# Squares of the residual in tiles of their own, in the output projection of a hybrid decoder layer

## The chip, the cores and the metric

One core of a Trainium2 chip runs the whole layer as one program. The metric is the device time of that program in microseconds (us), the median of three runs. The engines named below are PE (matrix products), DVE and ACT (elementwise work), POOL (hardly used) and SP (it issues most of the loads). An engine works through its own queue in order; ACT's queue also carries the DMA issues that ACT makes.

## What is computed

The layer has 512 tokens of width 2048. What matters here is its middle:

```python
x = x + ycat.reshape(B, S, D_MIX) @ w_out[l]          # four branches, joined, one output projection
h = rmsnorm(x, norm_ffn_g[l])                          # needs the sum of squares of x over the 2048 features
x = x + (silu(h @ w_gate[l]) * (h @ w_up[l])) @ w_down[l]
```

## The kernel before

Everything is kept transposed: a tile is 128 features by 512 tokens, and x is 16 such tiles, `x2[0]` to `x2[15]`. Float32 products are done with three matmuls of rounded parts: a value is split into `hi` (ACT, a copy that rounds) and `lo` (DVE, the rest), for weights (`issue_split`, L122 on ACT and L123 on DVE) as for data (`split2`, L1057 on ACT and L1058 on DVE).

The program order is written out by hand, and each engine keeps it. The output projection comes in two parts. The first (L1022) adds three branches to x. The second is the loop over `g` from 0 to 7 that the diff touches. Each `g` takes one weight chunk of 128x4x256 and computes two blocks of x, `g` and `g + 8`, here called a pair, with 24 matmuls (L162 to L164), 12 for a block. Before its matmuls `next_chunk` splits the chunk of the pair after it, so the split of chunk g+1 stands at the head of pair g in the queues of ACT and DVE, behind everything of pair g-1. The three raw weight buffers and four split buffers are shared by turns.

When a block is done, `on_last` runs `make_x2` (L1047): DVE adds the product to x2 (L1048), ACT scales it by the norm's gain into `xg` (L1050), ACT's queue issues a DMA that stores x2 to DRAM (`xd`, L1051; it is read again near the end of the layer), and ACT squares x2 in place (L1053). Behind the second block of a pair come `split_a11` (half of xg, rounded on ACT and subtracted on DVE), `add_squares` (L1043, DVE: one add of the two oldest tiles of squares), and `first_sums(g - 1)` (L1071, L1072, L1078 on DVE, with a split of the result between them: L1057 on ACT, L1058 on DVE). At g = 6 the first gate weights are split as well (`w_split(0)`).

Then come the gate and up projections, in 11 groups of weights, each by a recursive scheme of seven products P1, P5, P6, P3, P7, P4, P2 with 48 matmuls each, in four steps of 12 (`strassen`, L1244 to L1246). At each step DVE and ACT form sums of raw weights (`w_sum`, L1135 to L1147) and split them (`w_split`), two to three steps ahead. Between half steps the generators in `side` advance by one: `late_sums` makes the other sums of xg (first group only), and `ffn_norm` adds up the remaining tiles of squares, one add for each half step, then sums them over the partitions with matmuls against a column of ones (`norm2.add`, L229, on PE) and takes the root (L234, L235). The norm's factor `norm2.r` is first read at the end of P4 (L1202). The tiles named here come from one pool of 79 buffers.

The products P1, P6, P7 and P4 accumulate in the same PSUM banks, and the partial results are taken out in between: by ACT (L1199) after P1, P5 and P6, by DVE after P3 (L1211) and P7 (L1213). The next product on these banks waits for that.

Of the kernel before, what the change touches and what calls it, by code (L numbers as in the profile page):

```python
# [10 lines left out]
AF = mybir.ActivationFunctionType  # L11
# [28 lines left out]
def hybrid_kernel(ctx, tc, xT, wi, wt, wo, wgu, wdn, vec, rows, sgw, w2a2, g2, pbias, cmask, oneh, addc, out):  # L40
    nc = tc.nc
    pe, dv, ac, gp = nc.tensor, nc.vector, nc.scalar, nc.gpsimd
# [11 lines left out]
    def t2(name, shape=(128, 512), dt=F32):  # L54
        return p2.tile(list(shape), dt, name=name, tag="s2")
# [94 lines left out]
    def gemm(nchunk, rhs, on_block):  # L150

        acc = [None, None]
        for c in range(nchunk):
            hi, lo = next_chunk()
            for b in range(2):
                if c == 0:
                    acc[b] = pm(f"acc{b}")
                for k in range(4):
                    xh, xl = rhs(c, k)
                    wh = hi[:, k, b * 128:(b + 1) * 128]  # L160
                    wl = lo[:, k, b * 128:(b + 1) * 128]
                    pe.matmul(acc[b], wh, xh, start=(c == 0 and k == 0), stop=False)  # L162
                    pe.matmul(acc[b], wh, xl, start=False, stop=False)  # L163
                    pe.matmul(acc[b], wl, xh, start=False, stop=(c == nchunk - 1 and k == 3))  # L164
                if c == nchunk - 1:
                    on_block(b, acc[b])
                yield
# [49 lines left out]
    def vcol(i):  # L217
        return vc[:, i:i + 1]
# [732 lines left out]
    def run(g, n=1):  # L951
        for _ in g:
            step_side(n)
# [57 lines left out]
    x2 = {}  # L1011
# [25 lines left out]
    sqs = []  # L1037
    cmb = {}

    def add_squares(sqs=sqs, cc=slice(0, S)):  # L1040
        if len(sqs) > 1:
            t = sqs.pop(0)
            dv.tensor_add(sqs[0][:, cc], t[:, cc], sqs[0][:, cc])  # L1043
# [3 lines left out]
    def make_x2(j, acc):  # L1047
        dv.tensor_add(x2[j], acc, x2[j])  # L1048
        xg[j] = t2("xg")
        ac.activation(xg[j], x2[j], AF.Copy, scale=vcol(V_NFG + j))  # L1050
        nc.scalar.dma_start(xd[j], x2[j])  # L1051
        sqs.append(x2.pop(j))
        ac.activation(sqs[-1], sqs[-1], AF.Square)  # L1053

    def split2(hi, src, lo):

        ac.activation(hi, src, AF.Copy)  # L1057
        dv.tensor_sub(lo, src, hi.bitcast(F32))  # L1058

    def split_a11(j):  # L1060
        a11 = t2("a11", dt=F32R)
        split2(a11[:, lo_t], xg[j][:, lo_t], a11[:, hi_t])
        cmb["P1", j] = a11[:, lo_t], a11[:, hi_t]
# [3 lines left out]
    def first_sums(j):  # L1067

        a, b = xg[j], xg[j + 8]
        s12 = s2[j] = t2("s12")  # L1070
        dv.tensor_add(s12[:, lo_t], a[:, hi_t], b[:, hi_t])  # L1071
        dv.tensor_sub(s12[:, hi_t], s12[:, lo_t], a[:, lo_t])  # L1072
        h12, l12 = t2("h12", dt=F32R), t2("l12", dt=F32R)
        split2(h12, s12, l12)
        cmb["P5", j] = h12[:, lo_t], l12[:, lo_t]
        cmb["P6", j] = h12[:, hi_t], l12[:, hi_t]

        dv.tensor_sub(s12[:, lo_t], b[:, lo_t], s12[:, hi_t])  # L1078
# [21 lines left out]
    def ffn_norm():  # L1100
        while len(sqs) > 1:
            add_squares()
            yield
        norm2.add(sqs.pop(0))
        norm2.root()
        yield
# [10 lines left out]
    def w_dma(limit):  # L1117
        while sw["dma"] < min(limit, len(steps)):
            gi, p, jj = steps[sw["dma"]]
            if p in FRESH:  # L1120
                if len(raw) + 2 > RAWS:
                    return
                kh, f = FRESH[p]
                for j in (2 * jj, 2 * jj + 1):
                    t = raw[kh, f, j] = t2("wq")
                    nc.sync.dma_start(t, wgu[gi, kh, f, j])
            sw["dma"] += 1
# [21 lines left out]
    def w_split(k):  # L1149
        gi, p, jj = steps[k]  # L1150
        hi = wp.tile([128, 2, 512], F32R, name="wh", tag="wraw", bufs=3)
        lo = wp.tile([128, 2, 512], F32R, name="wl", tag="wsp", bufs=4)
        if p in ("P5", "P6", "P4"):
            split2(hi, src.pop(k), lo)
        else:
            for u, j in enumerate((2 * jj, 2 * jj + 1)):
                q = {"P1": (0, 0), "P3": (1, 1), "P7": (1, 1), "P2": (1, 0)}[p] + (j,)
                split2(hi[:, u], raw.pop(q) if p in ("P7", "P2") else raw[q], lo[:, u])
        cut[k] = hi, lo
# [96 lines left out]
    for g in range(8):  # L1256
        def on_last(b, acc, g=g):
            make_x2(g + 8 * b, acc)
            if b:
                split_a11(g)  # L1260
                add_squares()
                if g:
                    first_sums(g - 1)
                if g == 4:
                    w_dma(4)
                if g == 6:
                    w_split(0)
                    sw["add"] = sw["split"] = 1
        run(gemm(1, lambda c, k: (yh[0, k], yl[0, k]), on_last))
    for f in range(4):  # L1270
        del yh[0, f], yl[0, f]
    side.append(late_sums())
    side.append(ffn_norm())


# [181 lines left out]
```

## Time and profile before

| | us |
|---|---|
| median of 3 runs (2360.51 to 2361.64) | 2361.01 |
| the profiled execution | 2362.09 |
| its span | 2360.3 |
| PE busy | 2280.0 (97%) |
| DVE busy | 1408.9 (60%) |
| ACT busy | 934.1 (40%) |

A stretch of the trace is given in us from the start of the span. The loop over g runs from about 873 to 970; group 0 of the gate and up projections follows it. The granted clock (PEclk) is a share of TensorE's full speed: 1.00 is 2.4 GHz, 0.50 is 1.2 GHz. Rows of waits name the engine that waited, its line, and the work that ended the wait.

### The profile page before, as it was taken

What the parts mean: (1) busy time and instruction counts of PE and PEld (TensorE: products, weight loads), DVE (VectorE), ACT (ScalarE), POOL (GpSimd) and SP (SyncE); (2) the same over time, 40 slices, a digit from 0 to 9 for tenths busy, and PEclk for the clock granted to TensorE, in tenths of its full rate; (3) what the DMA queues carried; (4) which work ended last, traced back from release to release, by engine and by line L of the source; (5) the groups of instructions that cost most, each with busy time, mean ns of one, the idle gap of its engine ahead of it and who ended that gap; (6) DMA issues with size and microseconds to landing.
All of it is one profiled execution on the core that took longest, in us unless ns stands there. A gap on an engine that the chain in (4) does not pass through costs nothing.

```text
span 2360.3 us, 29410 instructions
## 1 busy us (share of the span) xinstructions
PE 2280.0 (97%) x11404; PEld 1844.0 (78%) x11404; DVE 1408.9 (60%) x2250; ACT 934.1 (40%) x1465; POOL 2.3 (0%) x16
## 2 busy tenths in 40 slices
PE   8999999999999995699999999999999899999997
PEld 6788878877777774478888888888888788888887
DVE  6555456654444443688687868787878534434336
ACT  5522222243454433354544554455445422222223
POOL 0000000000000000000000000000000000000000
PEclk9999999999999997799999999999999999999999
DMA  5232323233233233234454545354534534434332
GB/s 186 86 91 74 100 75 92 60 99 90 63 100 114 89 104 117 93 124 157 134 165 132 159 134 170 125 161 134 165 129 166 195 99 134 128 96 133 116 116 90
DMA packets 144379, 283.00 MB, mean 120 GB/s; under 512 B 26544, under 2 KB 43440, under 8 KB 144240
## 3 DMA queue, kind: packets, MB, share of 16 engines
q1 hardware_dynamic: 124208, 255.12, 34.6%
q10 hardware_dynamic: 20032, 26.01, 3.3%
q8 instruction: 89, 1.46, 0.3%
q14 instruction: 50, 0.41, 0.1%
HBM read 260.33 MB, written 20.75 MB: 119 GB/s over the span
## 4 chain that ended last, share of the span: by engine, by line
PE 89%; DVE 5%; DMA 3%; ACT 2%; issue 1%; ACTq 0%; SPq 0%; DVEq 0%
PE acc L162 13%; PE acc L164 13%; PE acc L163 13%; PE prod L1244 11%; PE prod L1246 11%; PE prod L1245 11%; PE acc L180 3%; PE acc L182 2%; PE acc L181 2%; DMA xd<-x 2%; DVE wl L1058 1%; PE ph L1187 1%; PE po L898 1%; PE psc L833 1%; PE ppt L848 1%; PE acc L1361 1%
## 5 line engine op out<-in xcount | busy, mean ns | idle before, releaser
L123 DVE TENSOR_TENSOR wlo<-wraw,whi 128x1024 fp32r<-128x1024 f32 x207 | 253.2, 1224 | 300.4 <-ACT whi L122 300.2
L122 ACT ACTIVATE whi<-wraw 128x1024 fp32r<-128x1024 f32 x207 | 218.8, 1057 | 537.4 <-PE acc L163 431.7
L1058 DVE TENSOR_TENSOR wl<-wq,wh 128x512 fp32r<-128x512 f32 x352 | 227.3, 688 | 116.0 <-ACT wh L1057 114.8
L1245 PE MATMUL prod<-wl,h 128*128 128x512 f32 x704 | 274.7, 390 | 0.8 <-DVE wl L1058 0.8
L1244 PE MATMUL prod<-wh,h 128*128 128x512 f32 x704 | 274.7, 390 | 0.0
L1246 PE MATMUL prod<-wh,l 128*128 128x512 f32 x704 | 274.4, 390 | 0.0
L1057 ACT ACTIVATE wh<-wq 128x512 fp32r<-128x512 f32 x352 | 201.4, 623 | 165.0 <-PE prod L1246 108.4
L162 PE MATMUL acc<-hhi,whi 128*128 128x512 f32 x640 | 250.3, 391 | 2.4 <-ACT whi L122 2.4
L164 PE MATMUL acc<-hhi,wlo 128*128 128x512 f32 x640 | 250.1, 391 | 0.0
L163 PE MATMUL acc<-hlo,whi 128*128 128x512 f32 x640 | 250.0, 391 | 0.0
L162 PE MATMUL acc<-xhi,whi 128*128 128x512 f32 x512 | 209.5, 409 | 5.1 <-ACT whi L137 5.1
L164 PE MATMUL acc<-xhi,wlo 128*128 128x512 f32 x512 | 201.1, 393 | 1.0 <-DVE wlo L123 1.0
L163 PE MATMUL acc<-xlo,whi 128*128 128x512 f32 x512 | 201.0, 393 | 0.3 <-DVE xlo L253 0.3
L1057 ACT ACTIVATE wh<-T 128x1024 fp32r<-128x1024 f32 x132 | 139.9, 1060 | 149.5 <-PE prod L1246 140.6
L1058 DVE TENSOR_TENSOR wl<-T,wh 128x1024 fp32r<-128x1024 f32 x132 | 161.6, 1224 | 41.9 <-ACT wh L1057 41.9
L1245 PEld LDWEIGHTS prod<-wl,h 128*128 128x128 f32 x704 | 132.6, 188 | 28.9 <-DVE wl L1058 1.3
L1246 PEld LDWEIGHTS prod<-wh,l 128*128 128x128 f32 x704 | 132.6, 188 | 27.6
L1244 PEld LDWEIGHTS prod<-wh,h 128*128 128x128 f32 x704 | 132.6, 188 | 27.5
L1244 PE MATMUL prod<-wh,hb 128*128 128x512 f32 x352 | 139.8, 397 | 6.7 <-DVE c L1213 6.7
L162 PEld LDWEIGHTS acc<-hhi,whi 128*128 128x128 f32 x640 | 120.8, 189 | 28.0 <-ACT whi L122 2.8
L164 PEld LDWEIGHTS acc<-hhi,wlo 128*128 128x128 f32 x640 | 120.7, 189 | 25.8 <-DVE wlo L123 0.8
L163 PEld LDWEIGHTS acc<-hlo,whi 128*128 128x128 f32 x640 | 120.8, 189 | 25.1
(284 smaller groups left out, 3841.4 us busy)
## 6 DMA issues: line engine op xcount, KB each, us to landing
wq<-in_wgu_dram SPq DMA_DIRECT2D x440, 256.0 KB, 3.3
wraw<-in_wdn_dram SPq DMA_DIRECT2D x88, 512.0 KB, 3.5
wraw<-in_wi_dram SPq DMA_DIRECT2D x63, 512.0 KB, 3.6
wraw<-in_wt_dram SPq DMA_DIRECT2D x32, 512.0 KB, 3.6
wraw<-in_wo_dram SPq DMA_DIRECT2D x32, 512.0 KB, 3.5
hd<-hT ACTq DMA_DIRECT2D x44, 256.0 KB, 3.4
hraw<-hd SPq DMA_DIRECT2D x44, 256.0 KB, 4.8
xraw<-in_xT_dram SPq DMA_DIRECT2D x16, 256.0 KB, 5.5
```

Source lines behind the costliest of these rows:

```text
L122: ac.activation(hi, r, AF.Copy)
L123: dv.tensor_sub(lo, r, hi.bitcast(F32))
L162: pe.matmul(acc[b], wh, xh, start=(c == 0 and k == 0), stop=False)
L163: pe.matmul(acc[b], wh, xl, start=False, stop=False)
L164: pe.matmul(acc[b], wl, xh, start=False, stop=(c == nchunk - 1 and k == 3))
L180: pe.matmul(acc[i], th_, hi[:, k], start=(c == 0 and k == 0), stop=False)
L181: pe.matmul(acc[i], th_, lo[:, k], start=False, stop=False)
L1057: ac.activation(hi, src, AF.Copy)
L1058: dv.tensor_sub(lo, src, hi.bitcast(F32))
L1244: pe.matmul(acc[t], ah[:, tt], hi[:, u], start=first, stop=False, skip_group_check=more)
L1245: pe.matmul(acc[t], ah[:, tt], lo[:, u], start=False, stop=False, skip_group_check=more)
L1246: pe.matmul(acc[t], al[:, tt], hi[:, u], start=False, stop=(j == 7), skip_group_check=more)
```

## The change

Squaring leaves `make_x2` and becomes a function of its own that writes a new tile and lets go of x2. It is called for both blocks of a pair behind `split_a11` and `first_sums`; the add of squares comes last, and not at g = 0. In `ffn_norm` eight empty half steps stand between the last add and the matmuls of the column sums.

```diff
@@ make_x2
         ac.activation(xg[j], x2[j], AF.Copy, scale=vcol(V_NFG + j))
         nc.scalar.dma_start(xd[j], x2[j])
-        sqs.append(x2.pop(j))
-        ac.activation(sqs[-1], sqs[-1], AF.Square)
+
+    def square_x2(j):
+        sqs.append(t2("sq"))
+        ac.activation(sqs[-1], x2.pop(j), AF.Square)
@@ ffn_norm
         while len(sqs) > 1:
             add_squares()
             yield
+        for _ in range(8):
+            yield
         norm2.add(sqs.pop(0))
         norm2.root()
@@ on_last
             make_x2(g + 8 * b, acc)
             if b:
                 split_a11(g)
-                add_squares()
                 if g:
                     first_sums(g - 1)
+                square_x2(g)
+                square_x2(g + 8)
+                if g:
+                    add_squares()
                 if g == 4:
                     w_dma(4)
```

## Rows read from the trace of the kernel before

**Rows 1.** Windows: each engine's busy us (instructions), granted clock, DMA share, GB/s.

```profile
873.00:970.43 97.43, 60.03 (x193) 42.81 (x191) 39.16 (x68) 35.55 (x58) 0.00 (x0) 0.79 0.36 116
970.43:1042.04 71.61, 58.89 (x236) 47.16 (x235) 63.27 (x100) 35.07 (x55) 0.00 (x0) 0.88 0.34 104
908.00:912.00 4.00, 3.96 (x9) 3.14 (x10) 1.18 (x2) 0.72 (x1) 0.00 (x0) 0.50 0.74 184
1042.00:1130.00 88.00, 86.68 (x389) 71.47 (x390) 66.66 (x95) 42.67 (x63) 0.00 (x0) 1.00 0.41 132
```

**Rows 2.** Waits from 870 to 1010: us in total, times, longest.

```profile
DVE a L1058 <- ACT a L1057: 50.9, 8, 9.4
ACT x L1053 <- DMA xd<-x: 34.0, 16, 4.2
...
PE pacc L229 <- DVE x L1043: 9.0, 1, 9.0
```

**Rows 3.** Timeline of ACT, pair 2: start, us, instruction [idle before <- what ended it].

```profile
895.73 0.72 ACT L1050 ACTIVATE xg<-x,vc 128x512 f32<-128x512 f32 x1 [2.01 <-DVE x L1048]
...
900.05 0.63 ACT L1053 ACTIVATE x<-x 128x512 f32<-128x512 f32 x1 [3.60 <-DMA xd<-x]
...
900.59 0.71 ACT L1050 ACTIVATE xg<-x,vc 128x512 f32<-128x512 f32 x1
902.21 0.63 ACT L1053 ACTIVATE x<-x 128x512 f32<-128x512 f32 x1 [0.92 <-DMA xd<-x]
902.75 0.40 ACT L1057 ACTIVATE a<-xg 128x256 fp32r<-128x256 f32 x1
905.04 0.63 ACT L1057 ACTIVATE h<-s 128x512 fp32r<-128x512 f32 x1 [1.89 <-DVE s L1072]
905.57 1.04 ACT L122 ACTIVATE whi<-wraw 128x1024 fp32r<-128x1024 f32 x1
```

**Rows 4.** Timeline of DVE, pair 2 and the start of pair 3.

```profile
895.01 1.28 DVE L1048 TENSOR_TENSOR x<-acc,x 128x512 f32<-128x512 f32 x2
903.18 0.43 DVE L1058 TENSOR_TENSOR a<-xg,a 128x256 fp32r<-128x256 f32 x1 [6.89 <-ACT a L1057]
903.52 0.68 DVE L1043 TENSOR_TENSOR x<-x,x 128x512 f32<-128x512 f32 x1
904.12 0.42 DVE L1071 TENSOR_TENSOR s<-xg 128x256 f32<-128x256 f32 x1
...
905.70 0.69 DVE L1058 TENSOR_TENSOR l<-s,h 128x512 fp32r<-128x512 f32 x1 [0.70 <-ACT h L1057]
...
906.77 1.22 DVE L123 TENSOR_TENSOR wlo<-wraw,whi 128x1024 fp32r<-128x1024 f32 x1
907.90 1.28 DVE L1048 TENSOR_TENSOR x<-acc,x 128x512 f32<-128x512 f32 x2
```

**Rows 5.** Timeline of DVE: starts of pairs 0, 1, 7, and two marks in group 0.

```profile
873.00 0.69 DVE L1048 TENSOR_TENSOR x<-acc,x 128x512 f32<-128x512 f32 x1 [0.63 <-PE acc L164]
875.72 0.69 DVE L1048 TENSOR_TENSOR x<-acc,x 128x512 f32<-128x512 f32 x1 [2.03 <-PE acc L164]
...
882.01 1.28 DVE L1048 TENSOR_TENSOR x<-acc,x 128x512 f32<-128x512 f32 x2
...
959.20 1.28 DVE L1048 TENSOR_TENSOR x<-acc,x 128x512 f32<-128x512 f32 x2
...
970.43 2.50 DVE L1058 TENSOR_TENSOR wl<-wq,wh 128x512 fp32r<-128x512 f32 x4
...
1042.04 1.29 DVE L1213 TENSOR_TENSOR c<-prod,c 128x512 f32<-128x512 f32 x2
```

**Rows 6.** Timeline of PE: the first and the third matmul of a pair's chunk.

```profile
906.67 0.80 PE L162 MATMUL acc<-yhi,whi 128*128 128x512 f32 x1 [4.71 <-ACT whi L122]
...
908.04 0.79 PE L164 MATMUL acc<-yhi,wlo 128*128 128x512 f32 x1 [0.15 <-DVE wlo L123]
```

**Rows 7.** Waits of PE from 1042 to 1500: us in total, times, longest.

```profile
PE prod L1244 <- DVE c L1213: 4.6, 6, 2.4
```

## Prediction

> **What bounds the kernel now.** I read the page first: TensorE is busy 97% of the span, and the slices show one place where its busy share and granted clock fall together, the loop of the diff. So the time can only move there; elsewhere the matrix work itself is the length. The windows view of that place shows how much is open: from 873 to 970.43 PE works 60.0 of 97.4 us at a mean clock of 0.79, and from 970.43 to 1042.04 58.9 of 71.6; behind 1042 it works 86.7 of 88 us at full clock [rows 1]. PE's idle time up to 1042 is 37.4 + 12.7 = 50.1 us, and no edit here can save much more than that.
>
> The view of waits says who holds the loop. The longest wait is DVE's on ACT (50.9 us over the eight pairs), but ACT is itself waiting: 34.0 us in 16 waits of the in-place square for the store of the same tile, the longest 4.2 us [rows 2]. The square overwrites what the store is still reading. In one pair of the timeline the first square starts 4.3 us after xg (3.60 idle) and the second has 0.92 idle [rows 3]. Everything of the pair stands behind them on ACT: the rounding of a11, that of the sums, and the split of the next weight chunk, for which PE then waits (4.71 us before a first matmul) [rows 6]. So the loop is a ring, DVE add, xg, store, square, a11, sums, weight split, and back to the DVE add, and PE hangs beside it. The reader should see that DVE's two adds of the next pair come directly behind the weight subtraction [rows 4]: PE has long finished.
>
> **The change part by part: pairs 1 to 6.** The square no longer overwrites, so both store waits leave the ring; squares and the add of squares stay on their engines but at other places. I lay the ring out again with the start-to-start distances of the timeline, zero at the first DVE add of a pair:
> - The second add is over at 1.28, and ACT starts an xg 0.03 behind an add [rows 3, 4]: the second xg at about 1.32 (the first, started at 0.72, is out of the way).
> - A square of 0.63 lets the next instruction start 0.54 later; for an xg of 0.71 I take 0.62. a11 starts at 1.94, its DVE half 0.43 later, 2.37 [rows 3, 4].
> - The first sum follows 0.34 behind it, 2.71. Before, the add of squares stood between them (903.52 to 904.12, 0.60); it is now behind. From the first sum to ACT's rounding of the result are 0.92: 3.63 [rows 3, 4].
> - The two squares now stand here: 0.53 behind the rounding, 4.16, then 4.70; the weight split at 5.24. It ends 1.04 later, and the weight subtraction starts at 6.31, the next pair's add 1.13 behind that: **7.44** [rows 3, 4].
> - DVE is ready sooner: 0.66 from the rounding to its subtraction, 1.07 from there to the weight subtraction, and 0.60 for the add of squares, 5.96. The add of squares takes the two oldest tiles, never a fresh one, so it adds no wait.
>
> Is PE still beside the ring? Its first matmul starts when the weight split ends (6.28) and the third when the weight subtraction ends (7.53). 12 matmuls at full clock take 2.72 (873.00 to 875.72) [rows 5]; the 22 from the third on take 5.0, so both blocks are done at 12.5, where the ring asks for the first block at 14.9. That leaves about 2 us for a slow start.
>
> Pairs 1 to 6 took 959.20 - 882.01 = 77.19 [rows 5]. Six times 7.44 is 44.64: **32.55** saved.
>
> **Pair 0.** Its adds are set by PE at 873.00 and 875.72 [rows 5]. Without the waits xg follows at 876.44, a11 at 877.06, squares at 877.37 and 877.91, the split at 878.45, its subtraction at 879.52, the add of pair 1 at 880.65 in place of 882.01: **1.36** saved.
>
> **Pair 7** has no chunk to split; behind it come the gate weights. From its add to their first subtraction were 970.43 - 959.20 = 11.23 [rows 5]. By the same ring DVE gets there at 5.96 (ACT's rounding, 5.24 + 0.6, is just in time): **5.27** saved. To here 39.18.
>
> **Group 0 up to P7.** DVE works 63.3 of 71.6 us there [rows 1], so it stays the pace up to 1042.04, where PE waits for its add of P7's result, up to 2.4 us [rows 5, 7]. That queue is moved as a whole, by 39.18. One add more is in it (seven left before, eight now, since pair 0 has none): minus **0.60** [rows 4]. PE's wait of 9.0 us for the last add before the column sums [rows 2] goes, but I count it at nothing: PE then waits for the split weights of P5 and P6 instead, which come at DVE's pace. With its cover gone it would have cost the whole 9.0. The eight empty half steps put the column sums into P6, still three products ahead of their first reader in P4. The stores themselves, and the loads behind them on SP, are the same in number and order. A new tile is needed for each square; x2's buffer is given back at once, so one or two more of the 79 are in use. I count that at nothing; from both sides: no tile gained or lost, 0; a wait as long as the store's, at most 4.2 from xg's end [rows 2], is a rival below.
>
> **Sum.** 39.18 - 0.60 = **38.6 us**. The profiled execution (2362.09, span 2360.3) would become 2323.5; it lies 1.1 above the median of the runs, and from that, 2361.0, I get **2322.4**. Unseen are the distance behind an xg (0.62, between 0.54 and 0.72) and the handing over between engines after the reordering; 0.3 in each of six rings is 2 us, and with the slow starts of PE below I give this case 2318 to 2328.
>
> **The rivals.**
> 1. **TensorE's clock becomes the bound.** PE starts a chunk at 0.50 behind a pause of 4.71 us, nine matmuls in 4 us [rows 1, 6], about 0.43 each against 0.227. If it stayed there a whole chunk, 22 matmuls behind the third take 9.5, the second block is done at 17.0 and is asked for at 15.5: 1.5 for each of seven pairs, 10, and some 2.5 in P5 and P6, where PE would be late for P3. Saved 26: **2335**. For it: PE will pause about 1.1 us in each ring and 2 to 4 us in P1 to P6. Against it: behind the pause of 2.4 us at 1042 the clock stays 1.00 [rows 1, 7], and a slow start of 4 us is covered. [...]
> 2. **The wait returns by the buffers.** If x2's buffer is handed out again at once, the second square, or the next xg, waits for the store of the first. The store lands at most 4.9 behind its issue (xg's 0.72 and the wait of 4.2) [rows 2, 3]: 0.72 + 4.9 = 5.6 against 4.70, 0.9 in a ring; eight pairs cost 7.5: **2330**. For it: buffers do go round. Against it: with 24 tiles alive at the loop's start, 55 others are free ahead.
> 3. **PE alone is the bound.** If DVE's queue up to P7 closes up, all 50.1 us of idle PE go: **2311**. Against it: DVE's gaps there (8.3 us) are its own waits for ACT's rounding, which stay.
> 4. **Nothing changes**: the loads of gate weights, not the loop, set group 0, and its end stays at 1042: **2361**. Against it: no wait on them is among the long ones, and the DMA share is 0.34 to 0.36 [rows 1].
> 5. **Slower.** The denser loop no longer lets TensorE recover at all: short bursts keep it at 0.50 from pair 2 to the end of P7. Then six chunks take 24 x 0.43 = 10.3 in place of 7.44, 17 more, and the 240 matmuls of P1 to P7 103 us against DVE's 72, 31 more: 48 - 38.6 = 10 slower, **2371**. It decides from the point where slow matmuls cost more than 38.6, in the second half of P3. Against it: the slow spell of rows 6 ended within its own chunk.
>
> **How the numbers follow.** Forecast 0.70, rival 1 0.12, rival 2 0.07, rival 3 0.06, rival 4 0.02, rival 5 0.03. A measurement of this kernel can tell about 0.2% (4.7 us) from no change. All of the first four cases are faster by more: 0.95; same 0.02; slower 0.03. The range of the forecast, widened at the top to most of rival 2 and halfway to rival 1 and at the bottom towards rival 3, is 2315 to 2332.
>
> **What would show it.** In the profile of the changed kernel no store should be named among the long waits; the first adds of successive pairs should lie 7.2 to 7.8 apart, not 12.9; the weight subtraction should follow two squares on ACT; PE should wait for split weights in P1 to P6 and not for the add of squares; DVE's add of P7's result should lie near 1003.5. A distance of about 9 with PE named before the adds is rival 1, a wait of a square or of xg for a store is rival 2. The prediction is wrong if the pairs close up but the add of P7 does not move with them.

## The result and the profile after

The changed kernel takes **2323.97 us** (median of 4 runs, 2323.41 to 2325.93) against 2360.76 for the kernel before in the same comparison (4 runs, 2359.76 to 2361.64): a ratio of 0.9846 with an interval of 0.9829 to 0.9863. The forecast was 2322.4. The profiled execution takes 2323.97 with a span of 2321.9, where the one before took 2362.09 with 2360.3: the span is 38.4 us shorter.

The windows of the kernel after, over the loop, over group 0 up to the first partial sum added behind P7 (DVE's `c` at 1003.99), and over the 9 us from just before that add; the columns are those of [rows 1]:

```profile
874.36:932.39 58.03, 47.03 (x193) 34.90 (x191) 39.01 (x68) 33.40 (x57) 0.00 (x0) 1.00 0.57 182
932.39:1003.99 71.60, 60.08 (x236) 46.03 (x236) 63.74 (x103) 35.40 (x56) 0.00 (x0) 0.93 0.36 114
1002.99:1011.99 9.00, 7.17 (x25) 5.77 (x26) 5.84 (x7) 2.12 (x2) 0.00 (x0) 0.81 0.00 0
```

The loop is 58.0 us long in place of 97.4, with the same 193 matmuls, and the granted clock in it is 1.00 in place of 0.79. Group 0 is as long as before (71.60, 71.61). Its mean clock is 0.93, so TensorE ran slow for a part of it, as in the kernel before (0.88). The third line shows something that wasn't there before: behind P7's add the mean is 0.81, so here, too, TensorE ran for a part of the time at the lower of its two levels, 1.2 GHz in place of 2.4.

The longest waits of all engines from 870 to 1010 (who waited, for whom, us in total, times, longest):

```profile
ACT h L1059 <- DVE s L1088: 21.9, 8, 3.7
ACT xg L1050 <- DVE x L1048: 17.5, 9, 2.6
PEld prod L1249 <- DVE wl L1060: 14.0, 10, 2.5
DVE l L1060 <- ACT h L1059: 11.3, 16, 0.8
...
PE prod L1249 <- DVE wl L1060: 9.8, 8, 2.2
DVE a L1060 <- ACT a L1059: 8.9, 8, 1.1
```

No store is among them any more (34.0 us in 16 waits before), DVE's wait for a11 has gone from 50.9 to 8.9, and PE waits for split weights in place of the add of squares [rows 2].

The timeline of ACT after, pair 2 (start, duration, instruction, idle before):

```profile
890.17 0.72 ACT L1050 ACTIVATE xg<-x,vc 128x512 f32<-128x512 f32 x1 [1.89 <-DVE x L1048]
890.80 0.71 ACT L1050 ACTIVATE xg<-x,vc 128x512 f32<-128x512 f32 x1
891.41 0.40 ACT L1059 ACTIVATE a<-xg 128x256 fp32r<-128x256 f32 x1
893.09 0.63 ACT L1059 ACTIVATE h<-s 128x512 fp32r<-128x512 f32 x1 [1.28 <-DVE s L1074]
893.63 1.14 ACT L1055 ACTIVATE sq<-x 128x512 f32<-128x512 f32 x2
894.67 1.04 ACT L122 ACTIVATE whi<-wraw 128x1024 fp32r<-128x1024 f32 x1
```

And of DVE after, pair 2, with the starts of pairs 0, 1, 3 and 7 and the marks at the gate weights' first subtraction and P7's add:

```profile
874.36 0.69 DVE L1048 TENSOR_TENSOR x<-acc,x 128x512 f32<-128x512 f32 x1 [0.63 <-PE acc L164]
...
882.00 1.28 DVE L1048 TENSOR_TENSOR x<-acc,x 128x512 f32<-128x512 f32 x2
...
889.45 1.28 DVE L1048 TENSOR_TENSOR x<-acc,x 128x512 f32<-128x512 f32 x2
891.84 0.43 DVE L1060 TENSOR_TENSOR a<-xg,a 128x256 fp32r<-128x256 f32 x1 [1.11 <-ACT a L1059]
892.18 0.42 DVE L1073 TENSOR_TENSOR s<-xg 128x256 f32<-128x256 f32 x1
...
893.76 0.69 DVE L1060 TENSOR_TENSOR l<-s,h 128x512 fp32r<-128x512 f32 x1 [0.70 <-ACT h L1059]
...
894.83 0.68 DVE L1043 TENSOR_TENSOR sq<-sq 128x512 f32<-128x512 f32 x1
895.75 1.23 DVE L123 TENSOR_TENSOR wlo<-wraw,whi 128x1024 fp32r<-128x1024 f32 x1 [0.23 <-ACT whi L122]
896.89 1.28 DVE L1048 TENSOR_TENSOR x<-acc,x 128x512 f32<-128x512 f32 x2
...
926.41 1.28 DVE L1048 TENSOR_TENSOR x<-acc,x 128x512 f32<-128x512 f32 x2
...
932.39 2.49 DVE L1060 TENSOR_TENSOR wl<-wq,wh 128x512 fp32r<-128x512 f32 x4
...
1003.99 1.28 DVE L1217 TENSOR_TENSOR c<-prod,c 128x512 f32<-128x512 f32 x2
```

Pairs 2 and 3 start 896.89 - 889.45 = 7.44 us apart. Beside [rows 3, 4] the reader sees a11 directly behind the second xg, the first sum directly behind a11's subtraction, and the squares between the rounding and the weight split, without idle time before them.

Subtracting these marks, beside those of [rows 5], gives the account, in us:

| stretch | before | after | saved | predicted |
|---|---|---|---|---|
| pair 0 | 9.01 | 7.64 | 1.37 | 1.36 |
| pairs 1 to 6 | 77.19 | 44.41 | 32.78 | 32.55 |
| pair 7 to the gate weights | 11.23 | 5.98 | 5.25 | 5.27 |
| group 0 to P7's add | 71.61 | 71.60 | 0.01 | -0.60 |
| sum | 169.04 | 129.63 | 39.41 | 38.6 |

Outside it, the loop starts 1.36 later in this execution (874.36, 873.00), in work that the change doesn't touch; in another execution of the same changed kernel it starts at 873.65. From P7's add in group 0 to that in group 1 are 80.37 in place of 78.80, and from P7's add of the last group to the end 528.49 in place of 530.37.

### The profile page after: what moved, and what is told of

The parts are those of the page before. It is cut to its first block, busy times and chain, and to the rows that moved or that the text cites. A ratio compares the mean times of both kernels' runs of the same rounds, so it can differ in the third digit from the quotient of the medians.

```text
span 2321.9 us, 29403 instructions
## 1 busy us (share of the span) xinstructions
PE 2268.4 (98%) x11404; PEld 1834.9 (79%) x11404; DVE 1409.0 (61%) x2250; ACT 932.4 (40%) x1465; POOL 2.3 (0%) x16
## 3 DMA queue, kind: packets, MB, share of 16 engines
q8 instruction: 89, 1.46, 0.3%
## 4 chain that ended last, share of the span: by engine, by line
PE 91%; DVE 5%; ACT 2%; DMA 1%; issue 1%; ACTq 0%; SPq 0%; DVEq 0%
PE acc L162 14%; PE acc L164 13%; PE acc L163 13%; PE prod L1248 11%; PE prod L1249 11%; PE prod L1250 11%; PE acc L180 3%; PE acc L182 3%; PE acc L181 3%; DVE wl L1060 1%; PE ph L1191 1%; PE po L898 1%; PE psc L833 1%; PE ppt L848 1%; DMA xraw<-in_xT_dram 1%; PE acc L1368 1%
```

## The experiments

The theory: the in-place square waited for the store, and ring and end move by what the new ring adds up to. Rivals: the new places of squares and adds did it, not the tiles; or the eight empty half steps, which take the column sums out of PE's way. Each kernel was timed in five rounds; the kernel before took 2361.47, 2362.32 and 2361.48 in the three comparisons.

**The tiles alone.** Kernel before, with a tile of its own for each square and every instruction at its old place:

```diff
-        sqs.append(x2.pop(j))
-        ac.activation(sqs[-1], sqs[-1], AF.Square)
+        sqs.append(t2("sq"))
+        ac.activation(sqs[-1], x2.pop(j), AF.Square)
```

> The kernel before with one edit: the squares go into new tiles, at their old place right behind the store's issue; the add of squares and the column sums stay where they were. Theory (the in-place square waits for the store that still reads the tile, and that wait was the loop's ring): no long wait for a store is left. The ring by the rows: xg 0.72, square 1.34, second xg 1.88, square 2.50, a11 3.04, its DVE half 3.47, add of squares 3.81, sums 4.41, rounding 5.33, weight subtraction 7.06, next pair 8.19, so pairs 8.2 apart in place of 12.9 and 7.44; about 5 us more than the changed kernel, 2329. PE's wait for the last add before the column sums is there again and costs nothing beyond that. Rival (the column sums' place is worth its 9 us): 2338. Rival (order, not tiles, made the gain): near 2361.

Measured: **2329.02**, ratio 0.9861 (0.9846 to 0.9876). ACT in pair 2 of this kernel:

```profile
890.76 0.62 ACT L1053 ACTIVATE sq<-x 128x512 f32<-128x512 f32 x1
891.29 0.71 ACT L1050 ACTIVATE xg<-x,vc 128x512 f32<-128x512 f32 x1
891.90 0.61 ACT L1053 ACTIVATE sq<-x 128x512 f32<-128x512 f32 x1
892.42 0.40 ACT L1057 ACTIVATE a<-xg 128x256 fp32r<-128x256 f32 x1
```

The squares stand where they stood and wait for nothing; six rings take 49.01 us, 8.17 each. This part of the change is worth 32.4 us by itself. PE still waits 9.0 us for the last add of squares, and group 0 to P7's add takes 71.74 all the same: PE's wait is covered, but for about 0.6 us that DVE waits behind it (see group 0 below).

**The order alone.** The changed kernel, its squares late but in place:

```diff
-        sqs.append(t2("sq"))
-        ac.activation(sqs[-1], x2.pop(j), AF.Square)
+        sqs.append(x2.pop(j))
+        ac.activation(sqs[-1], sqs[-1], AF.Square)
```

> The changed kernel, but the late squares overwrite x2 again; order, adds and empty half steps as changed. Theory: the wait is for the store's landing, so it shrinks to what is left of a landing 3.4 us behind the issue (4.16 - 0.72 for the first square, 4.70 - 1.34 for the second): with landings of 2.0 to 4.9, 0 to 1.6 in each of seven rings, pairs 7.4 to 9.0 apart, 2324 to 2335, likeliest 2328. Rival (a tile of its own is needed whatever the order): the waits of before come back, near 2361.

Measured: **2330.05**, ratio 0.9864 (0.9847 to 0.988). Waits of this kernel for a store, from 870 to 1010:

```profile
ACT x L1055 <- DMA xd<-x: 5.3, 6, 1.8
```

Of 34.0 us of store waits 5.3 are left: a square that comes 2 to 3 us later meets a store that is nearly over. Its rings are uneven (8.32 on average, between 7.18 and 10.41). So either half alone brings over 31 of the 37 us, because both take away the same wait; their gains don't add.

**Without the empty half steps.** The changed kernel, with the column sums directly behind the last add:

```diff
-        for _ in range(8):
-            yield
```

> The changed kernel without the eight empty half steps, so the column sums stand behind the last add at the end of P1 again. Theory (PE's 9 us there are covered by DVE's queue, which sets the pace up to P7): PE waits for the add of squares by name, DVE's add of P7's result stays 71.6 us behind the first gate weight subtraction, and the time stays at 2324, within 1. Rival (the empty steps carry part of the gain): up to 9 slower, 2333.

Measured: **2323.13**, ratio 0.9836 (0.9821 to 0.9851), level with the changed kernel. The wait that the steps were to take away is there, in this kernel's row of waits:

```profile
PE pacc L229 <- DVE sq L1043: 6.9, 1, 6.9
```

Group 0 to P7's add takes 72.64 here, 1.04 more than with the steps, so it isn't the 71.6 that I expected: behind the column sums DVE waits 0.54 for ACT's rounding of a weight sum, a wait that it doesn't have there in the changed kernel. But from 1 us before this kernel's P7 add on, the windows view shows the clock at 1.00:

```profile
1003.98:1012.98 9.00, 7.17 (x32) 5.95 (x33) 6.54 (x9) 3.27 (x4) 0.00 (x0) 1.00 0.00 0
```

The next interval between P7 adds is then 78.79, 1.6 shorter. The two nearly cancel: in the whole time the steps bring nothing that can be measured, and what they would bring at an equal clock behind P7, about 1 us by this stretch, is an estimate.

**The add of squares back ahead of the sums:**

```diff
                 if g:
+                    add_squares()
                     first_sums(g - 1)
                 square_x2(g)
                 square_x2(g + 8)
-                if g:
-                    add_squares()
```

> The changed kernel with the add of squares ahead of the first sums again (squares stay late, in their own tiles). Theory (the add is a link of the ring there, 0.60): pairs 8.04 apart in place of 7.44, seven times 0.60, 4 us slower: 2328. Rival (DVE's add is hidden beside ACT): 2324.

Measured: **2326.69**, ratio 0.9852 (0.9837 to 0.9867). In the DVE timeline of this kernel the add stands in the ring again, and its pairs lie 8.04 apart (888.78 to 896.82):

```profile
896.82 1.28 DVE L1048 TENSOR_TENSOR x<-acc,x 128x512 f32<-128x512 f32 x2
899.22 0.42 DVE L1060 TENSOR_TENSOR a<-xg,a 128x256 fp32r<-128x256 f32 x1 [1.11 <-ACT a L1059]
899.56 0.69 DVE L1043 TENSOR_TENSOR sq<-sq 128x512 f32<-128x512 f32 x1
900.17 0.42 DVE L1073 TENSOR_TENSOR s<-xg 128x256 f32<-128x256 f32 x1
```

0.60 a ring, as worked out from [rows 4]; this distance shows the price of the add. The total lost against the changed kernel is 2.7, too little to tell the two kernels apart by their intervals. It fits that this kernel, too, kept its clock behind P7 (7 x 0.60 - 1.6 = 2.6), but other stretches of the two executions differ by over 1 us as well.

**Squares behind the split.** If the ring is ACT's and DVE's hand-over, the squares still cost 1.04 in each (893.63 to 894.67). This kernel issues them behind the weight split, while DVE subtracts:

```diff
         def on_last(b, acc, g=g):
+            if not b and g:
+                square_x2(g - 1)
+                square_x2(g + 7)
             make_x2(g + 8 * b, acc)
             if b:
+                if g > 1:
+                    add_squares()
                 split_a11(g)
                 if g:
                     first_sums(g - 1)
-                square_x2(g)
-                square_x2(g + 8)
-                if g:
-                    add_squares()
```

(`ffn_norm` begins with the two squares that are left.)

> The changed kernel with one more move: the two squares of a pair are issued in the next pair, behind the split of the weight chunk and ahead of the next xg, and the add of squares stands between the DVE adds of a pair and a11's half. Theory (squares are still two links of the ring on ACT, 1.07; ACT idles 1.9 us between the weight split and the next xg, and DVE 1.1 us behind its two adds, so both fit there): rounding 3.63, weight split 4.17 to 5.21, weight subtraction 5.36 (now set by DVE), next pair 6.50. Six rings 0.94 shorter each less what PE holds up at the first, the last pair 0.6, one more add in group 0 minus 0.6: 5 to 6 us faster than the changed kernel, 2318.5. Rival (PE or its clock takes over as the bound of the ring): no gain or slower, 2324 or more.

Measured: **2318.95**, ratio 0.9815 (0.9801 to 0.9828). DVE in pair 3 of this kernel; the add of squares lies in the time in which DVE waits for xg and a11, and pairs are 6.52 apart:

```profile
894.61 1.28 DVE L1048 TENSOR_TENSOR x<-acc,x 128x512 f32<-128x512 f32 x2
895.81 0.68 DVE L1043 TENSOR_TENSOR sq<-sq 128x512 f32<-128x512 f32 x1
897.00 0.43 DVE L1060 TENSOR_TENSOR a<-xg,a 128x256 fp32r<-128x256 f32 x1 [0.51 <-ACT a L1059]
...
901.13 1.28 DVE L1048 TENSOR_TENSOR x<-acc,x 128x512 f32<-128x512 f32 x2
```

**The adds of group 0 on GpSimd.** The same, with the nine adds left for group 0 on the idle engine:

```diff
         while len(sqs) > 1:
-            add_squares()
+            t = sqs.pop(0)
+            gp.tensor_add(sqs[0], t, sqs[0])
             yield
-        for _ in range(8):
+        for _ in range(16):
             yield
```

> The kernel with the squares behind the split, and the nine adds of squares that are left in group 0 put on POOL, which is idle, with sixteen empty half steps ahead of the column sums. Theory (DVE's queue sets the pace up to P7 and each add there costs 0.60): 5.4 faster than the kernel with the squares behind the split, 2313. Rival (POOL and DVE disturb each other at the tile memory, or POOL's adds come too late for the column sums): no gain or slower, 2318 to 2325.

Measured: **2320.99**, ratio 0.9824 (0.981 to 0.9837): 8 us over what I expected, and no gain over the last kernel. GpSimd's timeline in this kernel, and then DVE's:

```profile
923.31 10.23 POOL L1107 TENSOR_TENSOR sq<-sq 128x512 f32<-128x512 f32 x7 [576.25 <-ACT xg L1050]
937.47 2.70 POOL L1107 TENSOR_TENSOR sq<-sq 128x512 f32<-128x512 f32 x2 [3.93 <-ACT sq L1055]
```

```profile
924.78 1.48 DVE L1073 TENSOR_TENSOR s<-xg 128x256 f32<-128x256 f32 x1
...
930.67 4.62 DVE L1060 TENSOR_TENSOR wl<-wq,wh 128x512 fp32r<-128x512 f32 x4
935.22 0.41 DVE L1073 TENSOR_TENSOR s<-xg 128x256 f32<-128x256 f32 x1
...
937.58 1.47 DVE L1080 TENSOR_TENSOR s<-xg,s 128x256 f32<-128x256 f32 x1
938.96 1.49 DVE L1088 TENSOR_TENSOR s<-xg 128x256 f32<-128x256 f32 x1
```

GpSimd had been idle for 576 us. It ran seven of its nine adds at once in pair 7, 10.23 / 7 = 1.46 each, and the last two in group 0. While it ran, a DVE sum of 0.42 took 1.48, and four weight subtractions 4.62 in place of 2.49; behind the seven, 0.41 again; beside the last two, sums took 1.47 and 1.49. From pair 7's add to the weight subtraction DVE needed 9.42, in the kernel without GpSimd 5.46. These are 3.96, 2.13 and 2.1 us more, together about the 8 us by which the expectation was missed: the rival that it named came. The Trainium skill, "SBUF — State Buffer", section "Who interferes with whom", says that a VectorE instruction with two SBUF inputs contends with a GpSimd instruction that reads SBUF; the trace agrees. Its 1.48 beside 1.46 would fit one DVE instruction for each of GpSimd's, which no run tests.

**The adds in DVE's gaps.** In place of another engine, the time in which DVE waits 0.70 for ACT's rounding in each split of sums:

```diff
-    def split2(hi, src, lo):
+    def split2(hi, src, lo, between=None):
         ac.activation(hi, src, AF.Copy)
+        if between:
+            between()
         dv.tensor_sub(lo, src, hi.bitcast(F32))
...
-        split2(h12, s12, l12)
+        split2(h12, s12, l12, add_squares)
...
-            split2(h34, s12, l34)
+            split2(h34, s12, l34, add_squares)
```

(On top of the kernel with the squares behind the split; `ffn_norm` no longer adds by itself.)

> The kernel with the squares behind the split, with one add of squares more in each pair and in each late sum, put on DVE between the second subtraction of a sum and the subtraction of its rounding, where DVE idles 0.70 waiting for ACT; no adds at half steps of their own. Theory (DVE's queue is the pace up to P7, an add of 0.60 costs nothing inside the gap of 0.70): the ring of a pair stays 6.5, all but two adds are done before group 0 and those two lie in gaps, so the nine adds of 0.60 leave DVE's queue: 5.4 faster than the kernel with the squares behind the split, 2313.5, and from the first four-fold weight subtraction to the add of P7's result 66.8 in place of 72.2. Rival (PE or ACT is the pace by then): 2317 to 2319.

Measured: **2311.78** (5 runs, 2311.6 to 2315.07), ratio to the kernel before 0.9792 (0.9779 to 0.9806). It beats the kernel that it builds on (2318.95) and the changed kernel timed beside it (2324.09, below). DVE's timeline in pair 3 of this kernel, and its marks at the gate weights and at P7's add:

```profile
897.00 0.42 DVE L1076 TENSOR_TENSOR s<-s,xg 128x256 f32<-128x256 f32 x1
897.34 0.69 DVE L1043 TENSOR_TENSOR sq<-sq 128x512 f32<-128x512 f32 x1
898.12 0.69 DVE L1062 TENSOR_TENSOR l<-s,h 128x512 fp32r<-128x512 f32 x1
...
925.32 2.49 DVE L1062 TENSOR_TENSOR wl<-wq,wh 128x512 fp32r<-128x512 f32 x4
...
992.04 1.28 DVE L1220 TENSOR_TENSOR c<-prod,c 128x512 f32<-128x512 f32 x2
```

From the second sum to the subtraction are 1.12 with the add between them, as many as in the changed kernel, where DVE is idle for 0.70 of them. Group 0 to P7's add shrinks from 72.17 in the kernel that it builds on (71.60 in the changed kernel) to 66.72: DVE set its pace, and the adds had been part of it.

**The changed kernel again**, beside it:

> The changed kernel once more beside it, for a comparison on the same chip: 2324, as before.

Measured: **2324.09**, ratio 0.9841 (0.9828 to 0.9854).

## Why the prediction was right

**The store wait.** The ring was read rightly: the tiles alone bring 32.4 us with everything at its old place.

**Pairs 1 to 6.** Every step of the new ring is met within 0.04: from the pair's first add (889.45) the second xg comes at 1.35 (worked out: 1.32), a11 at 1.96 (1.94), its subtraction at 2.39 (2.37), the first sum at 2.73 (2.71), the rounding at 3.64 (3.63), the first square at 4.18 (4.16), the split at 5.22 (5.24), its subtraction at 6.30 (6.31), the next pair at 7.44 (7.44). The six together take 44.41, 0.23 under 6 x 7.44, since the last of them is 7.19. The unseen distance behind an xg was 0.61, where 0.62 was taken.

**Group 0** holds the mis-sized term. The forecast took off 0.60 for one add more and counted the column sums' wait at nothing; measured, the stretch kept its length. The add does cost what was forecast: with the squares behind the split group 0 has nine adds in place of eight, and takes 72.17 in place of 71.60; with none in the way it takes 66.72, 0.61 less for each of the nine. What paid for it is part of the wait that was counted at nothing. The last step of the norm's root (L235) stands in DVE's queue behind the column sums. In the kernel before, DVE idled 0.59 for it, and in the changed kernel, behind the empty half steps, it doesn't; before, then after:

```profile
994.37 0.18 DVE L235 RECIPROCAL rn<-rn 128x4 f32<-128x4 f32 x1 [0.59 <-ACT rn L234]
```

```profile
975.02 0.17 DVE L235 RECIPROCAL rn<-rn 128x4 f32<-128x4 f32 x1
```

So the forecast asked what PE's wait of 9.0 us would cost, and not what DVE waits for behind the same sums. That PE's own wait was covered was right, and so was the place of P7's add: forecast near 1003.5, found at 1003.99.

**What was missing.** In the sum, 0.8 more was saved than forecast, in the ring and in group 0. Outside it, 1.9 less was spent behind the last group, against 1.36 more at the loop's start and 1.57 more behind P7. That the errors nearly cancel is luck, and the end is nearer than its parts. By the medians (2360.76, 2323.97) the change saved 36.8, 1.8 less than the sum; the profiled execution before, from which the stretches are read, took 1.3 longer than its median.

**The rivals.** The first, the clock, did not come in the loop. PE's timeline of the changed kernel, first matmuls of a pair's chunk:

```profile
895.77 0.50 PE L162 MATMUL acc<-yhi,whi 128*128 128x512 f32 x1 [0.93 <-ACT whi L122]
896.10 0.40 PE L163 MATMUL acc<-ylo,whi 128*128 128x512 f32 x1
897.03 0.50 PE L164 MATMUL acc<-yhi,wlo 128*128 128x512 f32 x1 [0.53 <-DVE wlo L123]
```

Pauses of up to 0.93 and of 0.53 in a ring leave the clock at 1.00 over the whole loop. The slow matmuls of [rows 6] stood behind a pause of 4.71. The Trainium skill, "TensorE: Matmul & The Clock Gate", section "HAM oscillation — how this bites in real kernels", tells of a kernel with waits of about 3 to 5 us between its bursts of matmuls, each of which starts cold; the pause of 4.71 agrees with it, and the pauses in the changed kernel's loop are shorter than those waits. The rival was near, though: in the kernel with the add of squares ahead of the sums, two chunks began behind pauses of 1.48 and 1.49, and the granted clock was 1.00 behind the one (904 to 908) and 0.70 behind the other (912 to 916). In group 0 of the changed kernel the clock did fall (0.50 from 948 to 952), where DVE sets the pace. Behind P7 it cost time: 25 matmuls where full speed gives 32 in the same 9 us, about 1.6 us. The second rival (the wait comes back through buffers) has no row: ACT waits for no store any more. The third (PE alone) did not come: PE still has 11.0 us idle in the loop and 11.5 in group 0. And its 50.1 us, which I had taken for all that could be saved, were not the ceiling: the same 193 matmuls of the loop keep PE busy for 47.03 us in place of 60.03, so what a low clock adds to busy time is to be had as well. The last experiment saves 49.7 with PE still idle in group 0. The fourth (nothing changes) and the fifth (slower) fell with P7's add at 1003.99.

## What to carry to other kernels

An in-place operation on a tile that a store still reads made its engine wait for the store here (34.0 us in 16 waits), and with it all that was queued behind it; give the result a tile of its own or issue the operation later, but don't count both, since they remove the same wait. When a loop is a ring through two engines, lay it out start to start, and then move whatever nobody waits for into the places where one engine waits for the other: here that brought another 12 us, while moving it to the idle third engine slowed the second.

## What the runs showed of the hardware

The pause of PE at P7's add is 2.40 us in the kernel before as in the changed one (1.8 in the GpSimd kernel). Over the 9 us from 1 us before that add, the granted clock is 1.00 in the kernel before and in four experiments, and 0.81 in the changed kernel in both its executions and in three others. It costs 1.6 us: from this add to the next group's are 78.8 us in the kernels at 1.00 and 80.2 to 80.4 in the others. What decides it no run tells apart. The stretch behind the last group's P7 add, too, varies from 528.5 to 530.5 over the kernels, though none of the edits reaches there; why stays open.

Beside GpSimd's adds a DVE sum took three and a half times as long (0.42, 1.48). I had named this as a rival without a size; it cost the experiment its gain.
